# Attention block, one core: the first three groups' probabilities by VectorE squares and transfers inside SBUF, the last stage's pools in another order, the gates' low parts one block sooner

## The chip, the cores and the metric

The kernel runs on one core of a Trainium2 chip. The metric is the device time of one execution in microseconds, the median of several. The engines are named as in the profile: PE (TensorE) multiplies matrices, DVE (VectorE), ACT (ScalarE) and POOL (GpSimd) work on tiles, SP (SyncE) issues most of the DMAs; POOL issues some of them too. PEld is the loading of weights into PE.

## The reference, cut to what matters

One layer over 4096 prompt rows (and 64 sample rows) of width 1024:

```
h = rmsnorm(x, g_pre);  z = h @ w_in                     # 2816 columns
cb, cc, ch, cg, q, k, v, ag, mq, mg = split(z)
out_a = silu(cg) * cb * conv3(cc * ch)                    # 256 columns
out_b = silu(ag) * window_attention(q, k, v, sink)        # 8 heads, 2 kv heads, window 128
out_c = silu(mg) * memory_attention(mq, mk, mv)           # 4 heads, 256 memory tokens
y = concat(out_a, out_b, out_c) @ w_out
x + rmsnorm(y, g_post)
```

The window attention goes by groups of 128 queries: group b sees the keys of its own 128 rows and of the 128 rows before (none for group 0), and a sink per head. All arithmetic keeps float32 accuracy: a product is made from high and low parts in three matmuls.

## The kernel before, in words

Four stages follow one another. In phases 0, 1 and 2 (`input_projection`) z is computed for blocks of 520 rows; in each block seven Strassen products (A11 to A22 in `PRODUCTS`), each over all column tiles of the phase, give the `c` matmuls of L374. The first two blocks of phase 0 are plain (`plain_block`, `plain_jobs`, eight steps each). Jobs are put between the products: loads, splits of the operands (`hi_x` on ACT, `lo_x` on DVE, L364 and L365), evictions (L381, L383, L417). PE, DVE and SP take their instructions in the order in which the program lists them.

Phase 2 has eight blocks of seven products, counted by n in `third_jobs(b, p)`: up to n = 12 the memory's keys and values, from n = 13 `first_chunk`, and then the attention of groups 0, 1 and 2, in pieces put between products. `wo_load` and `wo_split` in its last block bring w_out and split it into high parts (ACT) and low parts (DVE, `w_split`, L197).

The last stage is opened by `open_attention` (L1013), which makes its pools, and runs 32 prompt blocks and one block of the samples. A block is 48 `y` matmuls (out-projection of 128 rows), and between them, at places given by `events_of(i)`, the attention of the group three blocks ahead: scores (`ws`, `xs`), softmax, and the values (`pv`) of the group one block ahead. Groups come in chunks of two: `chunk_load(c)` loads a chunk's keys (`kst`) and queries (`q`) by POOL's DMA queue, `load_mix` its gates from `md` by SP's, for even chunks into `place`, for odd ones into `mix`.

A group's probabilities have queries in partitions; the values need keys there. For groups from 3 on the scores lie as squares of 32 columns: `turn_band` and `turn_cross` transpose 32x32 squares on DVE (STREAM_TRANSPOSE 128x1024 each), 16 DMAs of 32x512 on SP (`w<-s`, L1274) move the squares inside SBUF, `masks` zeroes what the window excludes (four affine selects on POOL, L1283), and `values` makes 32 matmuls: 16 for the memory (`pv<-w,mv`), 8 for the band (`pv<-w,vh`), 8 for its rest (`pv<-wd,vh`). The score buffer `s` of odd groups is single.

For groups 0 to 2 the probabilities are flat, and PE transposes them: 8 transposes for the band (`wt`), 8 for the memory (`xt`), copies out of PSUM on ACT or DVE (`wpt`, `xpt`, `w`), affine selects on POOL (L1296, L1298), then `early_values` with `wo` matmuls of 128x512 and 16 `xo` matmuls. Group 2's transposes stand in block 0 of the last stage, its values in block 1.

Further places that the change touches: `rows_product` (L311) spreads the normalisation factors of a block over partitions by PE, and ACT copies them to `rb` (L317); `rows_load` (L262) loads the factors of phase 1's first two blocks; `Block.split` (L1573, L1578) makes a block's high part `mh` on ACT and low part `ml` on DVE; the sample's window attention is done in four pieces among blocks 27 to 30.

## Time and profile before

| | us |
|---|---|
| median of 3 runs | 1496.32 (1494.26 to 1496.76) |
| profiled execution | 1497.36 |
| its span | 1495.6 |
| phase 2 begins, ends | 676.1, 953.5 |
| a block of the last stage without waits | 16.0 |

The profiled execution took 1.76 us beside its span, and 1.04 more than the median. Times in a timeline count from the span's start. A row such as "805.46 0.59 ACT L1292 COPY wpt<-wt 128x512 ..." gives the start, the duration, the engine, the line of the kernel, the operation, the tiles written and read, and in brackets, where there is one, the idle time before it with its inferred releaser. A row of a group gives the count, the busy time and the mean duration in ns, then the idle time. A row of the windows gives for each engine the busy time and the number of instructions, in the order PE, PEld, DVE, ACT, POOL, then the granted PE clock, the share of the DMA engines in use and GB/s. Matmuls overlap: what a piece of PE costs is read from its start to the start of the next.

### The profile page before, as it was taken

Reading aid. Unit: us, or ns where it says so; the run is one execution under the profiler, and the core shown is the slowest. Engines: PE = TensorE matmul, PEld = TensorE weight load, DVE = VectorE, ACT = ScalarE, POOL = GpSimd, SP = SyncE. Lnnn points to the kernel's source line nnn. Section 1 sums busy time; section 2 is a strip of 40 time slices with the busy share of each in tenths; the row PEclk is TensorE's granted clock in tenths of the full one; section 3 lists DMA queues with packets and bytes.
Section 4 is the critical chain, followed back from the end, with each engine's and each line's share of the span. In section 5 each row is a group of like instructions: output and inputs, shape, how many; then the busy total and the mean of one; then the engine's idle time right before and its main releaser. Section 6 shows DMA issues by size and latency. Waiting matters only on the chain.

```text
span 1495.6 us, 30807 instructions
## 1 busy us (share of the span) xinstructions
PE 1470.5 (98%) x11479; PEld 1343.0 (90%) x11479; DVE 1202.6 (80%) x1887; ACT 763.3 (51%) x1879; POOL 412.7 (28%) x553
## 2 busy tenths in 40 slices
PE   9999999999999999999999999999999999999998
PEld 9999999999999999999999999877777777778766
DVE  5779888898988877798667767968898888898853
ACT  5776655566422222244444534755655565665542
POOL 0222322212400000000000011235555656566631
PEclk9999999999999999999999999999999999999999
DMA  9989999886765432377967797989889998989662
GB/s 259 168 253 228 289 263 272 232 294 238 188 225 171 156 112 103 124 264 247 317 227 218 222 272 244 305 242 239 220 220 249 234 238 222 223 220 248 191 201 99
DMA packets 212363, 334.18 MB, mean 223 GB/s; under 512 B 54517, under 2 KB 126197, under 8 KB 212181
## 3 DMA queue, kind: packets, MB, share of 16 engines
q1 hardware_dynamic: 170117, 259.30, 57.8%
q0 software_dynamic: 40800, 69.76, 19.3%
q10 hardware_dynamic: 1296, 3.15, 0.7%
q8 instruction: 91, 1.49, 0.4%
q14 instruction: 59, 0.48, 0.1%
HBM read 192.54 MB, written 110.15 MB: 202 GB/s over the span
## 4 chain that ended last, share of the span: by engine, by line
PE 73%; DMA 11%; DVE 7%; issue 4%; SPq 3%; ACT 2%; POOL 1%; ACTq 0%; DVEq 0%; POOLq 0%
PE c L374 43%; PE y L66 19%; PE pv L66 4%; PE ws L66 2%; DMA nat<-in_x_p 2%; SPq L1274 2%; DMA place<-in_xt 2%; PE y L1601 1%; DMA place<-md 1%; PE xs L66 1%; DMA wr_3A<-in_w_in 1%; DMA o_yp<-xr 1%; DMA xr<-in_x_p 1%; PE mem_acc L790 1%; DMA md<-th 1%
## 5 line engine op out<-in xcount | busy, mean ns | idle before, releaser
L66 PE MATMUL y<-wo,mh 128*128 128x512 f32 x992 | 318.3, 395 | 0.0
L381 DVE TENSOR_TENSOR z<-c,z 128x520 f32<-128x520 f32 (+1 forms) x308 | 194.1, 643 | 84.5 <-PE c L374 83.9
L66 PEld LDWEIGHTS y<-wo,mh 128*128 128x128 f32 x992 | 186.3, 188 | 52.2 <-DVE wmx L66 5.0
L66 PE MATMUL y<-wo,ml 128*128 128x512 f32 x496 | 193.5, 390 | 1.0 <-DVE ml L66 1.0
L1211 ACT ACTIVATE s<-s,wnm 128x128 f32<-128x128 f32 x248 | 96.0, 388 | 41.9 <-DVE wnm L66 38.9
L66 PEld LDWEIGHTS y<-wo,ml 128*128 128x128 f32 x496 | 93.3, 188 | 19.5 <-DVE ml L66 1.4
L1236 POOL TENSOR_SCALAR s<-s,xrd 128x256 f32<-128x256 f32 x124 | 59.7, 497 | 156.5 <-DVE xrd L66 101.5
L1194 ACT COPY s<-ws 128x256 f32<-128x256 f32 x124 | 40.0, 377 | 96.5 <-PE ws L66 70.9
L1629 POOL TENSOR_TENSOR xr<-yn,xr 128x1024 f32<-128x1024 f32 x30 | 72.1, 2402 | 25.4 <-ACT yn L1628 22.4
L66 DVE STREAM_TRANSPOSE s<-s 128x1024 f32<-128x1024 f32 x58 | 70.9, 1236 | 3.0 <-POOL s L1236 3.0
L749 POOL MEMSET negs<- 128x1 f32 x1 | 0.1, 99 | 264.8 <-PE c L374 264.8
L1609 ACT ACTIVATE y<-y 128x512 f32<-128x512 f32 (+1 forms) x64 | 37.4, 584 | 54.0 <-DVE yn L66 46.6
L1283 POOL TENSOR_SCALAR_AFFINE_SELECT wd<-w 128x512 f32<-128x512 f32 (+1 forms) x56 | 51.7, 923 | 42.2 <-DMA w<-s 32.9
L66 DVE TENSOR_TENSOR yn<-y,gpost 128x512 f32<-128x512 f32 x62 | 42.3, 682 | 24.2 <-PE y L66 22.1
L1228 ACT ACTIVATE s<-xs,xnm 128x256 f32<-128x256 f32 x124 | 56.5, 462 | 4.1 <-DVE xnm L1226 3.2
L66 DVE COPY_PREDICATED s<-wmask,ws 128x256 f32<-128x256 uint8 x116 | 44.9, 441 | 16.2 <-ACT s L1194 10.4
L66 PEld LDWEIGHTS ws<-kst,q 64*128 64x128 f32 x696 | 44.5, 190 | 12.8 <-issue 10.2
L287 ACT ACTIVATE nat<-nat 104x1024 f32<-104x1024 f32 x40 | 42.2, 1057 | 25.9 <-DMA nat<-in_x_p 25.8
L66 PE MATMUL ws<-kst,q 64*128 64x256 f32 x696 | 51.1, 292 | 2.0 <-DMA q<-qd 1.9
L383 ACT COPY z<-c 128x520 f32<-128x520 f32 (+1 forms) x44 | 24.4, 554 | 51.8 <-PE c L374 48.8
L1628 ACT ACTIVATE yn<-yn,yst 128x1024 f32<-128x1024 f32 x31 | 35.6, 1150 | 24.9 <-POOL yst L1622 22.9
L415 ACT CAST zh<-z 128x520 fp32r<-128x520 f32 x56 | 33.3, 624 | 26.4 <-DVE z L381 22.6
(1013 smaller groups left out, 4995.6 us busy)
## 6 DMA issues: line engine op xcount, KB each, us to landing
w<-s SPq DMA_DIRECT2D x464, 64.0 KB
q<-qd POOLq DMA_DIRECT2D x32, 768.0 KB, 9.7
xr<-in_x_p SPq DMA_DIRECT2D x32, 512.0 KB
nat<-in_x_p SPq DMA_DIRECT2D x39, 416.0 KB
o_yp<-xr SPq DMA_DIRECT2D x31, 512.0 KB
md<-th POOLq DMA_DIRECT2D x48, 260.0 KB, 6.2
qd<-zh SPq DMA_DIRECT2D x48, 260.0 KB
qd<-z SPq DMA_DIRECT2D x48, 260.0 KB
```

Of the source, the lines that this page charges most:

```text
L66: return (lambda *args, **kw: tc.keep_in_program_order(fn(*args, **kw))) if on else fn
L287: S.activation(t[:RG], t[:RG], AF.Square, accum_out=r[:RG, i : i + 1])
L374: TE.matmul(bank[:, :HW], l, r, start=first and i == 0, stop=last and i == 3 * KH - 1)
L381: add = lambda dst, other: V.tensor_tensor(dst, c, other, op=ALU.add)
L1194: S.copy(to, squares(s3[:, :, P : 2 * P]))
L1211: S.activation(sm[:, h], sm[:, h], AF.Exp, bias=nm[:, h : h + 1], scale=SCALE, accum_out=den[:, h : h + 1])
L1228: S.activation(p[:, i], s[:, i].rearrange("p (a k j) -> p a k j", a=2, k=4), AF.Exp, bias=nm[:, i : i + 1], scale=SCALE, accum_out=den[:, ...
L1236: G.tensor_scalar(p[:, i], p[:, i], rd[:, i : i + 1], 0.5, op0=ALU.mult, op1=ALU.mult)
L1283: G.affine_select(out, src, pattern=[[32 * sign, 2], [0, 8], [sign, 32]], compare_op=op, fill=0.0, base=base * sign, channel_multiplier=-s ...
L1609: square = lambda acc=acc, p=p, c0=c0, c1=c1, end=end: S.activation((psum(2, "sq") if end else acc)[:m, : c1 - c0], acc[:m], AF.Square, sc ...
L1628: tc.keep_in_program_order(S.mul(yn, yn, st[:, 3:4]))
L1629: G.tensor_tensor(self.xr, yn, self.xr, op=ALU.add)
```

## The change

Groups 0 to 2 take the way of the other groups: squares, `turn_band` and `turn_cross` on DVE (together `early_turn`), 16 DMAs, `masks`, `values`. Their DMAs go by POOL's queue. A timetable `EARLY` says at which n of phase 2 each piece stands: group 0 has its scores from 15 to 18, its turn at 20, masks at 24, values at 26; group 1 scores 25 to 28, then 30, 34, 36; group 2 scores 36 to 39, turn 41, masks 45, and its values stay in block 1 of the last stage. Groups 0 and 1 write their values to two PSUM banks and multiply the gates in three pieces instead of two.

The low parts of wo for j = 9, 11, 13, 15 are made by POOL. Chunk 1 is loaded at n = 29. Chunk 3 is loaded in block 1 of the last stage and no longer in block 0, and `kst2` lies in another pool. The pools of the last stage are made in another order, so new tiles lie where other old tiles were and wait for other instructions; on SP the first load of x now stands ahead of the load of chunk 1's gates, which stood far ahead of it. In block 0, group 3's scores come at place 3 instead of 4. POOL keeps the listed order in blocks 1 and 2. From block 28 on the split of the next block moves from (1, 3) to (0, 6). `rows_product(2)` moves to the front of its step; `rows_load` of phase 1's second block moves from p = 1 to p = 0.

```diff
-    def w_split(w, raw):
+    def w_split(w, raw, engine=V):
         copy = S.copy(w[:, 0], raw)
...
-        V.tensor_tensor(w[:, 1], raw, f(w[:, 0]), op=ALU.subtract)
+        engine.tensor_tensor(w[:, 1], raw, f(w[:, 0]), op=ALU.subtract)
...
-        if p == 1 and nph == 1 and nb < PLAIN_BLOCKS:
+        if p == (0 if nb else 1) and nph == 1 and nb < PLAIN_BLOCKS:
             jobs.append(lambda: rows_load(nb, nb > 0))
...
-            (1, 5): lambda: [*fills(2, "S3"), lambda: rows_product(2), *fills(2, "S1"), *gains(2, "B21"), *fills(2, "S4"), *row],
+            (1, 5): lambda: [lambda: rows_product(2), *fills(2, "S3", "S1"), *gains(2, "B21"), *fills(2, "S4"), *row],
...
-        if n > 13 and third["chunk"]:
-            jobs.append(third["chunk"].pop(0))
-        elif n > 13 and len(chunks) == 1:
+        if n == 29:
             jobs.append(lambda: chunk_load(1))
-        elif n > 13 and early[0] < 4 and n >= 38:
-            if early[0] == 0:
-                groups[2] = Group(chunks[1], 0)
-            jobs.append(lambda u=early[0]: groups[2].early_scores(u))
-            early[0] += 1
+        for b, at in enumerate(EARLY):
+            if n == at[0]:
+                jobs.append(lambda b=b: groups.update({b: Group(chunks[b // 2], b % 2)}))
+            for fn in [fn for fn, m in zip(PIECES, at) if m == n]:
+                jobs.append(lambda b=b, fn=fn: fn(groups[b]))
...
+    EARLY = ((15, 16, 17, 18, 20, 24, 26), (25, 26, 27, 28, 30, 34, 36), (36, 37, 38, 39, 41, 45))
+    PIECES = (*(lambda g, n=n: g.early_scores(n) for n in range(4)), lambda g: g.early_turn(), lambda g: g.masks(), lambda g: g.values())
...
-        w_split(wo[k][h], wo_raw.pop(j))
+        w_split(wo[k][h], wo_raw.pop(j), G if j > 8 and j % 2 else V)
...
-        yq = ctx.enter_context(tc.tile_pool(name="yq", bufs=1, side="right"))
         vp = ctx.enter_context(tc.tile_pool(name="vp", bufs=4, side="right"))
-        yp = ctx.enter_context(tc.tile_pool(name="yp", bufs=2, side="right"))
-        bq = att.enter_context(tc.tile_pool(name="bq", bufs=1))
-        wp = att.enter_context(tc.tile_pool(name="wp", bufs=2))
-        wl = att.enter_context(tc.tile_pool(name="wl", bufs=1))
-        bp = att.enter_context(tc.tile_pool(name="bp", bufs=1))
-        mixp = att.enter_context(tc.tile_pool(name="mixp", bufs=1))
+        left = lambda name, bufs=1: att.enter_context(tc.tile_pool(name=name, bufs=bufs))
+        sp, bp, wd0 = left("sp"), left("bp"), left("wd0")
+        left("gap").tile([P, NS], F32, name="gap")
+        bq, yq, wl, wd1, mixp, yp = left("bq"), left("yq"), left("wl"), left("wd1"), left("mixp"), left("yp", 2)
+        wp = wd0, wd1
...
-            if c == 2:
-                self.kst = third["work"].tile([P, D], F32R, tag="u", name="kst2")[:, : 2 * (P + CT)].rearrange("p (a n) -> p a n", a=2)
-            else:
-                self.kst = self.pool().tile([P, 4, P + CT], F32R, tag="k", name=f"kst{c}")[:, :2]
+            odd = c == 0 or c % 2
+            self.kst = self.pool().tile([P, 2 if odd else 4, P + CT], F32R, tag="k", name=f"kst{c}")[:, :2]
...
         def turn_cross(self):
             part = self.squares[:, :, 256:]
-            tc.keep_in_program_order(V.transpose(part, part))
-            to = (wl if self.b % 2 else wp).tile([P, 4, 512], F32, tag="w", name=f"w{self.b}", bufs=1)
+            self.in_turn(V.transpose(part, part))
+            b = self.b
+            to = (wl if b % 2 and b > 1 else third["we"]).tile([P, 4, 512], F32, tag="w", name=f"w{b}")
             for g in range(4):
                 for k in range(4):
-                    DMA.dma_start(to[32 * k : 32 * k + 32, g], self.squares[32 * g : 32 * g + 32, k])
+                    (DMA if b > 2 else G).dma_start(to[32 * k : 32 * k + 32, g], self.squares[32 * g : 32 * g + 32, k])
...
+        def early_turn(self):
+            self.turn_band()
+            self.turn_cross()
...
-        if i == 2:
-            chunk_load(4)
+        if i in (1, 2):
+            chunk_load(i + 2)
...
-            at(0, 0, lambda: groups[2].transposes(0))
-            at(0, 3, lambda: groups[2].transposes(1))
             at(1, 0, weights, 3)
...
-        at(0, 0 if i else 4, values_and_scores, i)
+        at(0, 0 if i else 3, values_and_scores, i)
...
-            if i != 2:
-                at(0, 1 if i else 4, chunk_load, i // 2 + 3)
+            if i > 2:
+                at(0, 1, chunk_load, i // 2 + 3)
...
-                at(1, 3, blocks[i + 1].split)
+                at(*((1, 3) if i < 28 else (0, 6)), blocks[i + 1].split)
...
-        InOrder.on, InOrder.scalar, InOrder.gpsimd = i < 31, i == 0, i == 2
+        InOrder.on, InOrder.scalar, InOrder.gpsimd = i < 31, i == 0, i in (1, 2)
```

Removed with it: `early_transposes`, `transposes`, `band_transposes`, `cross_transposes`, the former `early_values` of a group and its flat branches in `open_scores`, `band_weights`, `cross_values` and `values`. Not shown: some loads of the last stage's opening that move by a place, and the sample's mask and value tiles, which lie in other pools.

More of the change, by code (lines that the diff above doesn't have):

```diff
@@ L862, in first_chunk @@
         third["work"] = right.enter_context(tc.tile_pool(name="work", bufs=1, side="right"))
+        third["we"] = right.enter_context(tc.tile_pool(name="we", bufs=1, side="right"))
         chunk_load(0)
@@ L865, in first_chunk @@
         chunk.load_mix()
-        third["chunk"] = [chunk.early_values]
-        for i in range(2):
-            pair = Group(chunk, i)
-            third["chunk"] += [lambda pair=pair, n=n, fn=fn: fn(pair, n) for fn, ns in (
-                (Group.early_scores, (0, 1, 2)), (Group.early_transposes, (0, 1)), (Group.early_values, (1,)),
-                (Group.early_scores, (3,)), (Group.early_transposes, (2, 3)), (Group.early_values, (3,))) for n in ns]
+        chunk.early_values()
     sums_at = {(0, 3 + i): pair for i, pair in enumerate(PHASES[1])}
@@ L1645, in hybrid_layer @@
     chunk_load(2)
-    for n in range(1, 4):
+    for n in range(2, 4):
         half_load(n)
```

150 lines of the change are left out of this document (47 added, 103 removed).

## The prediction

> **What bounds the kernel now.** I read the busy times first, then the matrix engine's (PE's) idle pieces in the timeline, then the windows of five microseconds around the opening of the last stage, then the chain of waits there.
>
> ```profile
> PE 1470.5 (98%) x11479; PEld 1343.0 (90%) x11479; DVE 1202.6 (80%) x1887; ACT 763.3 (51%) x1879; POOL 412.7 (28%) x553
> ```
>
> PE sets the end. A microsecond is won only by PE work taken out, by a PE wait that goes, or by full clock where it is now reduced. These are the PE waits that the change touches (number in front: when PE went on; in brackets: how long it had waited and for whom):
>
> ```profile
> 89.64 0.39 PE L374 MATMUL c<-hi_1B,w_2A 128*128 128x260 f32 x1 [2.40 <-ACT rb L317]
> 377.97 0.39 PE L374 MATMUL c<-lo_0B,w_0S 128*128 128x260 f32 x1 [0.40 <-DVE lo_0B L365]
> ...
> 804.79 0.63 PE L1291 MATMUL wt<-ident,s 128*128 128x128 f32 x4 [0.85 <-PE c L374]
> 858.41 0.63 PE L1291 MATMUL wt<-ident,s 128*128 128x128 f32 x4 [0.24 <-DVE s L1220]
> 909.25 0.39 PE L374 MATMUL c<-lo_6T,w_0S 128*128 128x260 f32 x1 [0.73 <-DVE lo_6T L365]
> 972.08 2.72 PE L66 MATMUL ws<-kst,q 64*128 64x256 f32 x22 [1.92 <-DMA q<-qd]
> 994.97 1.09 PE L66 MATMUL pv<-w,mv 128*64 128x128 f32 x16 [2.88 <-ACT y L1609]
> ...
> 1439.31 0.50 PE L66 MATMUL y<-wo,ml 128*128 128x512 f32 x1 [1.04 <-DVE ml L66]
> ```
>
> The two near 972 and 995 cost more than their idle time. In the windows the column after the busy times is the granted clock, then the DMA share:
>
> ```profile
> 970.00:975.00 5.00, 3.08 (x28) 2.93 (x28) 3.09 (x6) 1.51 (x5) 1.14 (x4) 0.71 1.23 350
> 975.00:980.00 5.00, 5.00 (x41) 3.26 (x39) 3.63 (x8) 4.13 (x17) 2.28 (x2) 0.95 1.17 370
> ...
> 995.00:1000.00 5.00, 4.96 (x35) 2.66 (x36) 3.26 (x8) 3.15 (x13) 3.67 (x5) 0.66 0.67 192
> ```
>
> Lost clock is the window times what the clock lacks: 5 × 0.29 + 5 × 0.05 = 1.7 us behind the first wait, 5 × 0.34 = 1.7 behind the second. So the first is worth 1.92 + 1.7 = 3.6, the second 2.88 + 1.7 = 4.6. The Trainium skill ("TensorE: Matmul & The Clock Gate", What's actually happening) says that the clock falls after at least one idle window of about 3.4 us; the trace differs, since waits of 1.92 and 2.88 us are each followed by a reduced clock. By that rule the two waits would be worth 4.8 us, not 8.2, and the forecast below about 2 us later; the rows decide.
>
> What ends the two waits:
>
> ```profile
> 958.60 1.70 POOL L1095 DMA_DIRECT2D q<-qd  x2 [27.88 <-DMA qd<-z]
> ...
> 993.75 1.51 POOL L1283 TENSOR_SCALAR_AFFINE_SELECT wd<-w 128x512 f32<-128x512 f32 x2 [8.46 <-DMA w<-s]
> 995.33 1.41 POOL L1283 TENSOR_SCALAR_AFFINE_SELECT w<-w 128x512 f32<-128x512 f32 x2
> ...
> 993.67 0.65 ACT L1194 COPY s<-ws 128x256 f32<-128x256 f32 x2 [6.84 <-DMA w<-s]
> ```
>
> ```profile
> 970.99 15.37 DMA place<-md
> ```
>
> The queries q2 are issued by POOL only at 958.60, into a full DMA (shares above 1), and arrive when PE has waited for them until 972.08. The second wait is a row of three: the load place<-md, 15.37 us long in the chain of waits, holds up the transfers w<-s of group 3 behind it on SP; ACT's score copy waits for them until 993.67 because it writes the buffer they read; PE waits for ACT's square behind that copy.
>
> **The change part by part.** *PE work of groups 0 to 2.* These rows give starts, so a piece lasts to the next row's start:
>
> ```profile
> 814.93 1.08 PE L1054 MATMUL wo<-wpt,mix_s 128*64 128x512 f32 x4
> 815.94 0.39 PE L374 MATMUL c<-hi_4B,w_0A 128*128 128x260 f32 x1
> ...
> 833.95 1.09 PE L1054 MATMUL xo<-xpt,mv 128*64 128x128 f32 x16
> 834.97 0.39 PE L374 MATMUL c<-hi_4T,w_2S 128*128 128x260 f32 x1
> ...
> 864.56 1.08 PE L1054 MATMUL wo<-s,mix_s 128*64 128x512 f32 x4
> 866.43 0.39 PE L374 MATMUL c<-hi_5T,w_2S 128*128 128x260 f32 x1
> ...
> 953.52 1.03 PE L66 MATMUL wt<-ident,s 128*128 128x128 f32 x8
> 954.39 0.60 PE L66 MATMUL xt<-ident,s 128*128 128x128 f32 x4
> 954.75 0.48 PE L66 MATMUL y<-wo,mh 128*128 128x512 f32 x1
> ...
> 975.81 1.09 PE L66 MATMUL pv<-w,mv 128*64 128x128 f32 x16
> 978.55 0.50 PE L66 MATMUL y<-wo,mh 128*128 128x512 f32 x1
> ...
> 1109.48 1.09 PE L66 MATMUL pv<-w,mv 128*64 128x128 f32 x16
> 1112.12 0.50 PE L66 MATMUL y<-wo,mh 128*128 128x512 f32 x1
> ```
>
> Sixteen transposes per group: eight take 954.39 − 953.52 = 0.87, four 0.36, so 0.87 + 2 × 0.36 = 1.59. Values now: group 0 takes 1.01 + 1.02 = 2.03, group 1 1.87 + 1.02 = 2.89, group 2 2.74. After, each group does what group 12 does at 1109.48, 2.64. Savings: 3.62 − 2.64 = 0.98; 4.48 − 2.64 = 1.84; 4.33 − 2.64 = 1.69. Together **−4.5**. With the transposes go the waits ahead of them, 0.85 + 0.24: **−1.1**.
>
> *What takes the transposes' place.* Per group two 128x1024 block transposes on DVE, 16 transfers inside SBUF issued by POOL, four masks on POOL. Rows of before for these, and for phase 2 as a whole:
>
> ```profile
> L66 DVE STREAM_TRANSPOSE s<-s 128x1024 f32<-128x1024 f32 x58 | 70.9, 1236 | 3.0 <-POOL s L1236 3.0
> 685.00:953.00 268.00, 265.66 (x2179) 256.10 (x2178) 197.39 (x312) 130.64 (x257) 20.06 (x26) 1.00 0.81 256
> L1095 POOL DMA_DIRECT2D q<-qd x30: 821/842/870, 718.4 to 1354.9; - x30
> ```
>
> DVE gains 6 × 1.24 = 7.4 us and is busy 197.39 of 268 us there, so it has room on the mean; each pair is still 2.5 us in front of whatever DVE does next, and the operand splits lo_x stand in that queue (909.25 shows PE waiting 0.73 for one). I charge one more wait of that size, **+0.6**; ends 0 and 7.4, all of it on the path. POOL is busy 20.06 of 268 us. Its issues take 0.84 each: 16 × 0.84 = 13.4. From the turn to the values the timetable leaves six products of about 5 us (some 54 in 268 us), 30 us; less 2.5 for the transposes, one product for DVE's queue, and 1.51 + 1.41 for the masks, about 20 us are left for 13.4. Hidden, at 0; if not, PE stands, because its order is fixed.
>
> The Trainium skill speaks against this move ("SBUF — State Buffer", SBUF: two separate sides): a DMA issued from GpSimd has its descriptors written by that engine, which is locked out while certain VectorE operations hold the shared port; it names 620 ns becoming 3100. The row of 30 issues agrees with no such thing: 821 to 870 ns, through phase 2 and the last stage, beside a DVE that is 74% busy. With 3100 ns the sixteen would take 50 us and PE would come about 30 us late twice; that is the third rival.
>
> *First wait of the last stage.* The order on POOL now has q2 ahead of kst2, without the wait for wo's splits on DVE that stands ahead of it now (the row of 958.60 names an older store), and chunk 3's loads behind block 0 instead of beside it. PE needs q2 at about 967 to 968, one set of transposes sooner than 972.08 − 1.92 = 970.16. Issued near 954 to 957 with the same 13 us it lands at 967 to 970, with less beside it sooner. I take the whole **−3.6**; ends −3.6 and 0. New here: kst2 comes behind q2, and four 128x512 splits of wo go to POOL, where the nearest row is a 128x1024 sum of 2.4 us:
>
> ```profile
> L1629 POOL TENSOR_TENSOR xr<-yn,xr 128x1024 f32<-128x1024 f32 x30 | 72.1, 2402 | 25.4 <-ACT yn L1628 22.4
> ```
>
> Half of it is 1.2 each; they are wanted by the second half of y, over 5 us into the block. I take 0; ends 0 and 4 × 1.2 = 4.8.
>
> *Second wait.* The first mix<-md and the xr loads of before on SP:
>
> ```profile
> L1103 SPq DMA_DIRECT2D mix<-md x8: 403/406/447, 961.3 to 1426.7; - x8
> ```
>
> ```profile
> 970.09 0.81 SPq L1558 DMA_DIRECT2D xr<-in_x_p  x2
> ```
>
> SP now issues xr0, then the mix of chunk 1, xr1, place, then w<-s. Group 3's softmax starts sooner (four copies on ACT and four splits on DVE fewer ahead of it), and place meets less traffic; but the load of mix, issued 9 us ahead of xr0 before, now stands directly ahead of it, and PE comes about 6 us sooner (the first wait's 3.6, 1.6 of transposes, and the values). The two nearly cancel. Ends −4.6 (gone) and 0; I take **−2.0**.
>
> *Small moves.* Phase 0's row product is now PE's first job, and the ACT copy rb goes ahead of one cast:
>
> ```profile
> 88.50 0.60 ACT L193 CAST w_2S<-wa2A 128x512 fp32r<-128x512 f32 x1
> 89.01 0.58 ACT L317 COPY rb<-rows_y 128x520 f32<-128x520 f32 x1
> ```
>
> That is 0.51 of the 2.40: **−0.5**. The row load of phase 1's second block stands about 2 us earlier on SP; it held DVE here, and PE behind it:
>
> ```profile
> 375.52 1.24 DVE L341 TENSOR_TENSOR x_1B<-x_1B,rb 128x1040 f32<-128x1040 f32 x1 [2.59 <-DMA rb<-rowd]
> ```
>
> PE's waits after it begin with 0.40 at 377.97 and are small and several; **−0.8**, ends −1.6 and 0. The low parts of the last prompt blocks come half a block sooner, which removes PE's wait for ml at 1439.31: **−1.0**. What they push back is the sample's softmax.
>
> The sum: −4.5 − 1.1 + 0.6 − 3.6 − 2.0 − 0.5 − 0.8 − 1.0 = −12.9. The profiled execution took 1497.36, 1.04 above the median of 1496.32, so 1497.36 − 12.9 − 1.04 = **1483.4 us**.
>
> **The rivals.** *The opening only exchanges its waits (0.25).* Against the forecast speak the DMA shares above 1 until 980 and the 15.37 us of one load: mix 1 is issued 9 us later than before and its gate multiply stands in DVE's order; if it too takes 15 us from 971 it lands near 986, and DVE and what follows are held. For it speaks that total bytes are unchanged. Then −3.6 and −2.0 are lost and up to 5 us are added: 1489.0 to 1494, taken as 1490.5. In this case the change does not do at the opening what its order says.
>
> *DVE becomes the bound of phase 2 (0.10).* It decides where a transposing pair meets a split lo_x that is due; all 7.4 us in place of 0.6 gives 1490.2. The 71 us of DVE idle time in the window speak against.
>
> *POOL's transfers come late (0.15): the slower side.* Place: PE's fixed order at the values of groups 0 and 1. It decides once one issue takes over 20 / 16 = 1.25 us. If a 1.24 us DVE operation holds up each 0.84 us issue, sixteen take 33.3, PE is 13 us late twice and loses 1.7 of clock each time: +29.4, so 1512.8. About 1.7 us per issue would already eat the whole gain.
>
> **How the numbers follow.** The forecast has 0.50. What a measurement can tell from no change is 0.2%, 3 us. Forecast: all faster. Exchange: 0.18 faster, 0.07 same. DVE: 0.06 faster, 0.04 same. POOL: slower. So 0.74, 0.11, 0.15. Low end: the second wait gone wholly (−2.6) and the row load's other 0.8 and a little of the charge of 0.6 bring 1479.5; high end: the exchange with nearly its whole addition, 1494. For the likeliest case alone 1479.5 to 1488.
>
> **What would show it.** No transposes and no idle before them at 805 and 858; PE's values of groups 0 and 1 with no wait for POOL; 16 POOL issues of w in under 14 us; the scores of block 1 starting without a wait for q; granted clock 1.00 behind it; a wait of 1 to 2 us for group 3 some 9 us earlier than 995; the row product's wait at 1.9. It is wrong if PE waits at the values in phase 2, or if DVE stands for the mix of chunk 1 until past 980.

## The result, and the profile after

The changed kernel is slower: 1501.97 us, median of 7 runs (1499.18 to 1508.01), beside 1496.08 for the kernel before (7 runs, 1494.26 to 1496.76). The ratio is 1.005, with a 95% interval of 1.0032 to 1.0067. The profiled execution took 1505.62, which is 3.65 above the median, and the two profiled executions, on which the sums below rest, lie 8.26 apart, while the medians lie 5.9 apart: the sums overstate the loss by some 2.4 us.

The busy times of the page of after answer to the first line of the prediction:

```profile
PE 1470.2 (98%) x11459; PEld 1343.8 (89%) x11459; DVE 1211.9 (81%) x1889; ACT 758.0 (50%) x1869; POOL 441.8 (29%) x607
```

By the page's count PE lost twenty instructions, and the span grew by 8.3. Where, is read from the windows by stage: phases 0 and 1, phase 2, the opening of the last stage up to the scores of block 5, the middle up to those of block 28, and the rest. Columns: window, length, busy time and instructions of PE, PEld, DVE, ACT and POOL, granted clock, DMA share, GB/s. After:

```profile
0.00:669.18 669.18, 665.13 (x5499) 663.26 (x5499) 554.60 (x762) 326.14 (x546) 104.10 (x166) 1.00 0.74 216
669.18:954.96 285.78, 277.58 (x2243) 267.50 (x2244) 214.02 (x336) 132.50 (x260) 52.26 (x83) 0.98 0.81 256
954.96:1041.46 86.50, 79.02 (x551) 62.92 (x549) 72.06 (x129) 47.92 (x175) 41.43 (x54) 0.98 1.05 269
1041.46:1413.77 372.31, 371.13 (x2689) 291.69 (x2688) 330.78 (x581) 222.44 (x808) 218.65 (x276) 1.00 0.89 225
1413.77:1503.90 90.13, 77.34 (x486) 58.42 (x485) 40.47 (x85) 29.01 (x82) 25.35 (x30) 0.94 0.44 141
```

The same windows of the kernel before:

```profile
0.00:676.14 676.14, 667.53 (x5499) 663.45 (x5499) 553.78 (x762) 325.12 (x546) 105.25 (x166) 1.00 0.73 214
676.14:953.52 277.38, 275.04 (x2255) 265.48 (x2255) 206.77 (x330) 135.10 (x265) 20.50 (x27) 1.00 0.80 253
953.52:1042.22 88.70, 83.76 (x559) 65.59 (x557) 70.71 (x133) 51.20 (x181) 41.61 (x55) 0.96 0.97 256
1042.22:1413.34 371.12, 370.17 (x2688) 291.88 (x2688) 329.85 (x580) 222.78 (x808) 220.17 (x275) 1.00 0.89 226
1413.34:1495.60 82.26, 73.98 (x486) 56.62 (x485) 41.52 (x85) 29.12 (x82) 25.16 (x32) 0.99 0.49 157
```

Idle time is the length less PE's busy time; lost clock is summed from windows of 5 us, each with 5 times what its clock lacks.

| stage | predicted | measured | of it PE idle | of it lost clock |
|---|---|---|---|---|
| phases 0 and 1 | −1.3 | −7.0 | −4.6 | 0 |
| phase 2 | −2.8 − 1.1 + 0.6 = −3.3 | +8.4 | +5.9 | +5.2 |
| opening | −1.7 − 3.6 − 2.0 = −7.3 | −2.2 | +2.5 | −1.7 |
| middle | 0 | +1.2 | +0.2 | 0 |
| end | −1.0 | +7.9 | +4.5 | +5.2 |
| sum | −12.9 | +8.3 | +8.6 | +8.7 |

What is left is 8.3 − 8.6 − 8.7 = −9.0. About 1.8 of it only corrects a double count: in after, windows over the waits themselves show that the clock was reduced by 1.41 us during the wait that ends at 1461.12, by 0.30 during the one at 943.54 and by 0.14 during the one at 994.47, where a slow clock costs nothing more. The other 7.2 or so is less PE work; 4.5 of it was counted from rows of work taken out, for the rest there is no row (ends of matmuls are modelled). So the work went as hoped, and more than all of it was paid back in waits and in the clock behind them. These are the waits, from PE's timeline of after (start, duration, what, and in brackets the idle time before it with its releaser), with the first row of group 0's values ahead of them:

```profile
832.04 1.09 PE L1046 MATMUL pv<-w,mv 128*64 128x128 f32 x16
...
863.62 0.39 PE L374 MATMUL c<-lo_5T,w_0S 128*128 128x260 f32 x1 [0.77 <-DVE lo_5T L365]
...
870.58 0.39 PE L374 MATMUL c<-lo_5B,w_0S 128*128 128x260 f32 x1 [2.36 <-DVE lo_5B L365]
...
941.65 0.39 PE L374 MATMUL c<-hi_7B,w_0S 128*128 128x260 f32 x1 [0.87 <-ACT hi_7B L364]
...
943.54 0.59 PE L374 MATMUL c<-lo_7B,w_0S 128*128 128x260 f32 x1 [1.51 <-DVE lo_7B L365]
...
971.31 1.70 PE L66 MATMUL ws<-kst,q 64*128 64x256 f32 x24 [2.69 <-issue]
...
994.47 1.76 PE L66 MATMUL pv<-w,mv 128*64 128x128 f32 x14 [4.79 <-DMA w<-s]
...
1461.12 1.97 PE L66 MATMUL pv<-w,vh 128*64 128x256 f32 x8 [5.87 <-POOL w L1248]
```

And the windows of after behind them, the granted clock third from the right:

```profile
870.00:875.00 5.00, 4.42 (x24) 4.42 (x25) 1.77 (x2) 0.95 (x1) 1.57 (x3) 0.66 1.08 288
...
940.00:945.00 5.00, 2.63 (x14) 2.22 (x13) 5.00 (x9) 3.57 (x5) 0.78 (x1) 0.79 1.03 381
945.00:950.00 5.00, 5.00 (x25) 5.00 (x25) 5.00 (x6) 2.62 (x5) 3.93 (x2) 0.52 0.50 174
...
1455.00:1460.00 5.00, 0.24 (x6) 0.00 (x1) 0.21 (x1) 1.84 (x3) 3.87 (x4) 0.84 0.27 100
1460.00:1465.00 5.00, 3.88 (x18) 1.84 (x19) 0.78 (x2) 0.00 (x0) 1.75 (x3) 0.50 0.37 125
```

The two small waits near 942 and 944, 2.38 us together, come with 5 × 0.21 + 5 × 0.48 = 3.45 of lost clock, 0.30 of it inside the second wait.

**What did not happen.** POOL's transfers are early. Its timeline for group 0:

```profile
810.79 6.99 POOL L1234 DMA_DIRECT2D w<-s  x14 [5.61 <-DVE s L1229]
...
824.19 1.54 POOL L1248 TENSOR_SCALAR_AFFINE_SELECT wd<-w 128x512 f32<-128x512 f32 x2 [4.04 <-DMA w<-s]
825.70 1.40 POOL L1248 TENSOR_SCALAR_AFFINE_SELECT w<-w 128x512 f32<-128x512 f32 x2
```

One issue takes 6.99 / 14 = 0.50 us, not the 0.84 assumed; the masks are done at 827.1 and PE begins the values at 832.04 without a wait. The transposes and their two waits are gone, and the 32 matmuls of a group take 2.48 us (832.04 to 834.52), a little under the 2.64 predicted.

**Where DVE is late in phase 2.** The wait at 870.58 is for `lo_5B`. DVE's timeline of after:

```profile
866.70 2.08 DVE L381 TENSOR_TENSOR z<-c,z 128x520 f32<-128x520 f32 x4 [2.79 <-PE c L374]
868.70 0.70 DVE L851 STREAM_TRANSPOSE vq<-vl 128x512 f32<-128x512 f32 x1
869.33 1.20 DVE L365 TENSOR_TENSOR lo_5B<-x_5B,hi_5B 128x1040 fp32r<-128x1040 f32 x1
```

ACT's timeline of after, for the high part it needs:

```profile
865.90 1.06 ACT L364 CAST hi_5B<-x_5B 128x1040 fp32r<-128x1040 f32 x1 [3.61 <-DMA x_5B<-hd_B]
```

And DVE's timeline of before, for the same piece of work:

```profile
874.63 1.23 DVE L365 TENSOR_TENSOR lo_5B<-x_5B,hi_5B 128x1040 fp32r<-128x1040 f32 x1
...
876.01 0.70 DVE L853 STREAM_TRANSPOSE vq<-vl 128x512 f32<-128x512 f32 x1
876.64 0.66 DVE L381 TENSOR_TENSOR z<-c,z 128x520 f32<-128x520 f32 x1
...
877.34 1.35 DVE L381 TENSOR_TENSOR z<-c,z 128x520 f32<-128x520 f32 x3
```

In after the split's input is there at 866.96, DVE had stood idle for 2.79 us until 866.70, and yet the split starts at 869.33: in the listed order it now stands behind four evictions and the transpose `vq` of the values, while before it stood ahead of all five. It starts 869.33 − 866.96 = 2.37 late, which is PE's whole wait of 2.36. DVE has room; what changed is who stands behind whom. SP's timeline of after has a similar row on the way of the load:

```profile
855.52 3.24 SPq L855 DMA_DIRECT2D vn<-vq  x4
858.81 2.33 SPq L525 DMA_DIRECT2D x_5B<-hd_B  x1
```

The stores `vn`, which wait for an earlier `vq`, take SP 3.24 us ahead of the load of `x_5B`. But they stood ahead of it before as well, at 2.29, so only about 1 us of this is new.

**Block 7.** Its two waits cost more than block 5's: 0.87 + 1.51 + 3.45 = 5.83, less the 0.30 counted twice, beside 0.77 + 2.36 + 1.70 = 4.83. Here it is a load that is late. SP issues `x_7B` at 932.63, behind six loads of w_out, and ACT, done with six casts of w_out, stands idle for 0.71 us until it has landed and begins its high part at 940.54. Issuing the six loads took SP 5.72 us, against 4.05 before; POOL issues group 2's transfers at the same time, from 920.39 to 930.10. DVE starts the low part at 942.26, behind two splits of wo, though the high part is ready at 941.60.

**Splits on POOL.** The four splits that left DVE saved it nothing. By line, before, then after (busy us, mean ns):

```profile
L197 DVE TENSOR_TENSOR wo<-wor,wo 128x512 fp32r<-128x512 f32 x16 | 10.6, 684 | 0.1
```

```profile
L197 DVE TENSOR_TENSOR wo<-wor,wo 128x512 fp32r<-128x512 f32 x12 | 11.6, 988 | 0.3 <-ACT wo L193 0.3
```

POOL's timeline of after has two of its four:

```profile
945.71 3.93 POOL L197 TENSOR_TENSOR wo<-wor,wo 128x512 fp32r<-128x512 f32 x2 [4.93 <-ACT wo L193]
```

So 1.96 us each for these two, not the 1.2 taken (the other two took 1.29 and 1.31), and DVE's own at 948.42 and 956.02, beside POOL's, took 1.77 and 2.16. The Trainium skill ("SBUF — State Buffer", Who interferes with whom) says that a VectorE instruction with both inputs in SBUF contends with a GpSimd instruction that reads SBUF. The trace agrees as far as DVE goes: its split at 956.02, beside POOL's from 956.31 to 957.62, took about three times the 684 ns that one took before. The prediction had weighed another section of the same page of the Trainium skill, on DMA issues that starve beside VectorE; of that the 48 issues show nothing.

**The end.** POOL's timeline of after before the wait of 5.87:

```profile
1456.06 0.55 POOL L1558 TENSOR_TENSOR yst<-yst,mhalf 128x1 f32<-128x1 f32 x1 [9.08 <-DVE yst L66]
1456.57 1.51 POOL L1248 TENSOR_SCALAR_AFFINE_SELECT wd<-w 128x512 f32<-128x512 f32 x2
1458.06 2.33 POOL L1565 TENSOR_TENSOR xr<-yn,xr 128x1024 f32<-128x1024 f32 x1
1460.35 1.40 POOL L1248 TENSOR_SCALAR_AFFINE_SELECT w<-w 128x512 f32<-128x512 f32 x2
```

And of before:

```profile
1451.53 1.52 POOL L1283 TENSOR_SCALAR_AFFINE_SELECT wd<-w 128x512 f32<-128x512 f32 x2 [4.85 <-DMA w<-s]
1453.11 1.41 POOL L1283 TENSOR_SCALAR_AFFINE_SELECT w<-w 128x512 f32<-128x512 f32 x2
1455.74 0.55 POOL L1622 TENSOR_TENSOR yst<-yst,mhalf 128x1 f32<-128x1 f32 x1 [1.22 <-DVE yst L66]
```

The masks of group 31, ahead of `yst` and `xr` before, now stand behind the one and on both sides of the other. POOL waits 9.08 us for a number of the block's norm that DVE has only at the block's end, and PE waits for the masks.

### The profile page after: what moved, and what is told of

Same layout as the page of the kernel before. It is cut to its first block, busy times and chain, and to the rows that moved or that the text cites. A ratio compares the mean times of both kernels' runs of the same rounds, so it can differ in the third digit from the quotient of the medians.

```text
span 1503.9 us, 30849 instructions
## 1 busy us (share of the span) xinstructions
PE 1470.2 (98%) x11459; PEld 1343.8 (89%) x11459; DVE 1211.9 (81%) x1889; ACT 758.0 (50%) x1869; POOL 441.8 (29%) x607
## 4 chain that ended last, share of the span: by engine, by line
PE 77%; DMA 6%; issue 6%; DVE 6%; ACT 2%; SPq 1%; POOL 1%; ACTq 0%; POOLq 0%; DVEq 0%
PE c L374 49%; PE y L66 18%; PE pv L66 4%; PE ws L66 2%; DMA w<-s 1%; PE xs L66 1%; DMA place<-md 1%; PE mem_acc L789 1%; SPq L1234 1%; ACT s L1193 1%; DMA x_5T<-hd_T 1%; DMA wr_3S<-sd6S 1%; DMA o_yp<-xr 1%; DMA vd<-v 1%; DMA x_7B<-hd_B 0%
## 5 line engine op out<-in xcount | busy, mean ns | idle before, releaser
L66 PEld LDWEIGHTS ws<-kst,q 64*128 64x128 f32 x696 | 43.1, 186 | 12.9 <-issue 12.9
L1248 POOL TENSOR_SCALAR_AFFINE_SELECT w<-w 128x512 f32<-128x512 f32 x60 | 48.9, 834 | 1.8
```

Source lines behind the costliest of these rows:

```text
L66: return (lambda *args, **kw: tc.keep_in_program_order(fn(*args, **kw))) if on else fn
L1248: G.affine_select(out, src, pattern=[[32 * sign, 2], [0, 8], [sign, 32]], compare_op=op, fill=0.0, base=base * sign, channel_multiplier=-s ...
```

## The experiments

Each is timed against the kernel before on the same chip; "tail" is the time from the scores of block 28 to the last matmul (75.85 before, 83.67 after), phase 2 was 277.38 and 285.78, the opening 88.70 and 86.50.

**e1_small.** The kernel before with both row moves:

```diff
-        if p == 1 and nph == 1 and nb < PLAIN_BLOCKS:
+        if p == (0 if nb else 1) and nph == 1 and nb < PLAIN_BLOCKS:
-            (1, 5): lambda: [*fills(2, "S3"), lambda: rows_product(2), *fills(2, "S1"), ...],
+            (1, 5): lambda: [lambda: rows_product(2), *fills(2, "S3", "S1"), ...],
```

> The kernel before with two of the change's moves alone: the row product first in its step, and the row load of phase 1's second block at p = 0. Theory: these two give all of the 7 us by which phase 2 starts sooner in the changed kernel (669.2 against 676.1), so the time is 1489 to 1491 and the waits of 2.40 us at 89.6 and of 2.59 us on DVE at 375.5 are gone. Rival: the prediction's sizes, 0.5 and 0.8 us (1495), the rest of the 7 us coming from the other pools and loads.

1491.25 beside 1495.45; ratio 0.9977 (0.9967 to 0.9987). The pair is worth 4.2 us (1.9 to 4.9 by the interval), not 1.3.

**e2_tail.** The changed kernel with the low parts back at (1, 3):

```diff
-                at(*((1, 3) if i < 28 else (0, 6)), blocks[i + 1].split)
+                at(1, 3, blocks[i + 1].split)
```

> The changed kernel with the split of blocks 29 and 30 back at its old place. Theory: the split at the new place delays the sample's softmax by 1.5 us, group 31's transfers with it, and in the listed order of POOL its masks then stand behind the yst and xr operations; back at the old place they stand ahead of them, the wait of 5.87 us at 1461 is gone and the time is 6.5 to 8 us less (1494 to 1495.5), with the 1.04 us wait for ml back. Rival: group 31's transfers are late for another reason (pools, DMA traffic), the wait stays over 4 us and the time within 2 us of the changed kernel's.

1501.81; ratio 1.0043 (1.0028 to 1.0058). In its profile the wait of 5.87 is gone and the tail is 78.06, with PE's wait for `ml` back (2.01 and 0.75), but the time hardly moves: its phase 2 took 287.48, 1.7 more than after. A miss in size: the two ratios differ by about 1 us, with an estimated interval from 4.5 in e2's favour to 2.4 against it, so the 4.8 that e5 finds below in the kernel before is not found again in the changed kernel's time. Why not is open.

**e3_split.** The changed kernel with all low parts of wo on DVE:

```diff
-        w_split(wo[k][h], wo_raw.pop(j), G if j > 8 and j % 2 else V)
+        w_split(wo[k][h], wo_raw.pop(j))
```

> The changed kernel with all low parts of wo on DVE again. Theory: POOL's subtracts and DVE's two-operand operations hold each other up (DVE's wo split took 2.16 and lo_7T 1.99 us beside them), and q2's second half waits behind POOL's last split; without them q2 and kst2 are issued 1 to 2 us sooner, the 2.69 us wait at 971 shrinks below 1 and the time is 2 to 4 us less (1498 to 1500). Rival: what holds q2 and kst2 is the full DMA, the wait at 971 stays over 2 us and the time within 1 us of the changed kernel's.

1500.64; ratio 1.004 (1.0026 to 1.0054), 1.3 below after, within the intervals of both. All sixteen splits on DVE now took 11.8 us, where twelve beside POOL's four took 11.6; so the move buys DVE next to nothing. PE's waits of the opening only change their places: 2.95 and 1.17 for the scores of block 1, 1.10 for group 3's values.

**e4_chunk.** The changed kernel with chunk 1 loaded at n = 33 instead of 29, to see whether its transfers delay `x_5B`:

```diff
-        if n == 29:
+        if n == 33:
```

> The changed kernel with chunk 1's keys and queries loaded at n = 33 instead of 29. Theory: the 1.9 MB of that load collide with the loads of x_5T and x_5B (landing 7 to 8.5 us after issue), so the waits of 0.77 and 2.36 us at 864 and 871 go and the time is 3 to 5 us less (1497 to 1499). Rival: the transfers of group 1 inside SBUF and the loads around them make the x loads late, the waits at 864 to 871 stay over 2 us in sum.

1503.68; ratio 1.0056 (1.0042 to 1.007). The waits near 864 and 871 are 0.77 and 2.35, as after. That theory fell.

**e5_tail_before.** The kernel before with the early split alone, the reverse of e2:

```diff
-                at(1, 3, blocks[i + 1].split)
+                at(*((1, 3) if i < 28 else (0, 6)), blocks[i + 1].split)
```

> The kernel before with one part of the change alone: the splits of blocks 29 and 30 at (0, 6). Theory: the split takes DVE and ACT ahead of the sample's softmax, group 31's transfers start 1.5 us later, and POOL's listed order puts its masks behind yst and xr: a wait of 4 to 6 us of PE at the values of group 31 and a reduced clock, 1.04 us for ml gained; the time is 3 to 7 us more than before. Rival: the tail of the changed kernel is made by its other parts; this one gains 1 us (1494 to 1495).

1500.76 beside 1495.93; ratio 1.0037 (1.0022 to 1.0051). One line costs 4.8 us; the wait of 5.87 stands in its profile, at 1460.30, and its tail is 82.81.

**e6_nodma.** The changed kernel with POOL copying instead of issuing the 48 transfers of groups 0 to 2. The transfers are left out, so the first 384 rows hold other values:

```diff
-                    (DMA if b > 2 else G).dma_start(to[32 * k : 32 * k + 32, g], self.squares[32 * g : 32 * g + 32, k])
+            if b > 2: ...
+            else:
+                G.tensor_copy(to, self.squares)
```

> The changed kernel without the 48 transfers of groups 0 to 2: one copy on POOL per group in their place, so the values of the first 384 rows are not the reference's. Theory that the transfers' traffic makes the x loads late: the waits at the operands 5T, 5B and 7B (7.4 us in sum in the changed kernel) fall under 3, the time is 4 to 7 us less. Rival, that the order of DVE and SP listed around them does it: lo_5B keeps its 2.35 us wait, since it stands behind four evictions there too, and the time is within 3 us of the changed kernel's.

1503.08; ratio 1.0048 (1.0035 to 1.0061). The waits at 5B and 7B are gone, but others stand in their place (1.45 for `lo_4B`, 1.56 and 1.45 for block 6), and phase 2 took 283.07, 2.7 less than after. The split of `lo_5B` is still late: its high part is ready at 867.32 and it starts at 870.73, behind the same evictions and `vq`; PE did not wait because group 1's values stood ahead of it. So the transfers are not what makes that split late. For block 7 the run excludes nothing: without the transfers its waits are gone, and the six w_out loads take SP 3.20 us instead of 5.72. The copies that POOL makes instead, 1.9 us each, are work of their own, so the time says little.

**e7_vturn.** The changed kernel with the values' loads and transposes (`vl`, `vq`, `vn`) one product sooner, so that `vq` and the stores behind it no longer stand ahead of a split:

```diff
-        if n >= 15 and n % 3 == 0 and n < 39:
-            jobs.append(lambda: v_load((n - 15) // 3))
-        if n >= 17 and n % 3 == 2 and n < 41:
-            jobs.append(lambda: v_turn((n - 17) // 3))
+        if n >= 14 and n % 3 == 2 and n < 38:
+            jobs.append(lambda: v_load((n - 14) // 3))
+        if n >= 16 and n % 3 == 1 and n < 40:
+            jobs.append(lambda: v_turn((n - 16) // 3))
```

> The changed kernel with the loads and transposes of the values' halves (vl, vq, vn) one product sooner. In this build no split lo_x stands behind evictions of the product before. Theory: the stores vn<-vq in SP's order hold back the loads x_5T and x_5B, and DVE's listed order around lo_5B costs the wait; both go, the waits of 0.77, 0.81 and 2.36 us at 863 to 873 fall under 1 in sum, and the time is 3 to 5 us less than the changed kernel's (1497 to 1499). Rival: DVE is simply short of time in phase 2 after the block transposes; the waits move to other splits and the time stays within 1.5 us.

1496.0 beside 1495.93; ratio 0.9999 (0.999 to 1.0008): 6 us won back. DVE's timeline of e7, to be held against after's at 866 to 869:

```profile
864.40 1.24 DVE L365 TENSOR_TENSOR lo_5B<-x_5B,hi_5B 128x1040 fp32r<-128x1040 f32 x1 [0.39 <-ACT hi_5B L364]
866.21 2.21 DVE L381 TENSOR_TENSOR z<-c,z 128x520 f32<-128x520 f32 x4 [0.56 <-PE c L374]
```

The split is ahead of the four evictions again and PE's waits there are gone. The edit also let SP issue `x_5B` ahead of the stores `vn`, so it does not part the two. Not all of the 6 us is this: phase 2 fell by 4.4 to 281.38, with waits of 3.51 and 1.64 left in block 7, and the tail fell by 5.5 to 78.14, since `yst` now came between the masks at 1449 and PE waited 2.88 for them. The opening took 1.6 more (waits of 4.26 and 2.91).

**e8_three.** e7 with e2's and e3's edits.

> The changed kernel with three parts mended: values' halves one product sooner, the splits of blocks 29 and 30 back, all low parts of wo on DVE. Theory: the three losses add up and are independent, so 1490 to 1494, under the kernel before. Rival: PE, when it comes sooner, meets the same loads at the opening and in block 7 of phase 2, and the time is 1497 or more.

1492.74; ratio 0.9977 (0.9969 to 0.9986), 3.3 below e7. What is left in phase 2 (280.90) is in block 7: a wait of 3.75 for `hi_7T` and one of 1.28 for `lo_7T`. PE's timeline of e8:

```profile
933.73 0.42 PE L374 MATMUL c<-hi_7T,w_0S 128*128 128x260 f32 x1 [3.75 <-ACT hi_7T L364]
```

And ACT's:

```profile
932.10 0.62 ACT L193 CAST wo<-wor 128x512 fp32r<-128x512 f32 x1 [0.22 <-DMA wor<-in_w_out]
932.62 1.05 ACT L364 CAST hi_7T<-x_7T 128x1040 fp32r<-128x1040 f32 x1
```

`x_7T` is issued at 918.68, beside group 2's transfers (915 to 926), and has landed at 928.43, when SP's next load into the same tile goes. Its high part begins only at 932.62, because ACT has three casts of w_out listed ahead of it (929.62, 931.26, 932.10), and each waits for its load. The first of these loads was issued at 920.44 and is used 9.2 us later; in the kernel before, which lists them in the same order, it is 5.6, and PE does not wait there. So it is the listed order again, this time on ACT, and behind it loads that group 2's transfers slow.

**e9_group2.** e8 with group 2 four products sooner, `EARLY[2] = (32, 33, 34, 35, 37, 43)`.

> e8_three with group 2's pieces four products sooner in phase 2 (scores 32 to 35, turn 37, masks 43), so its 16 transfers are over before the loads of w_out begin. Theory: these transfers and the first six loads of w_out make x_7T land 12 us after its issue; without them beside it PE's waits at 7T (3.75 and 1.28 us in e8_three) fall under 1.5 in sum and the time is 3 to 5 us less (1488 to 1490). Rival: the loads of w_out alone, ahead of x_7B and x_7T on SP, make the wait; it stays over 3 us.

1494.22 beside 1496.43; ratio 0.9982 (0.9966 to 0.9999). The wait of 3.75 in block 7 is gone (the first w_out load is used 5.7 us after its issue), but the scores of group 2 wait 4.58 for chunk 1's queries at 861.18, and phase 2 is as long (281.03).

**e10_place.** e8 with POOL issuing the first `place<-md`, to test the prediction's row of three at the second wait:

```diff
-            DMA.dma_start(self.mix, md[:, :, self.ts].rearrange("k p n -> p k n"))
+            (G if self.c == 2 else DMA).dma_start(self.mix, md[:, :, self.ts].rearrange("k p n -> p k n"))
```

> e8_three with the load of chunk 2's gates into place issued by POOL in block 1 instead of by SP ahead of group 3's transfers. Theory: the transfers w<-s on SP wait for the landing of place (12.5 us in the changed kernel); without it they end 4 us or more sooner, the wait at group 3's values (3.54 us) falls under 1 and the time is 3 to 5 us less (1488 to 1490). Rival: the transfers themselves are slow in the full DMA; they still end past 984, the wait stays over 2.5 us.

1493.79; ratio 0.9984 (0.9971 to 0.9997), no gain over e8. SP begins with w3's transfers at 966.62 and still takes 14.59 us over them (17.53 in after), and PE waits 3.40 for them. What the queue waits for, from the waits of SP between 964 and 992 (us in total, times, longest), in after:

```profile
SPq L1234 <- DMA place<-md: 3.9, 1, 3.9
```

And in e10:

```profile
SPq L1234 <- DMA xr<-in_x_p: 2.8, 1, 2.8
```

`place` does hold the transfers of `w` up, by 6.0 us in the kernel before, 3.9 in after and 3.4 in e8: the prediction's row of three is right. With `place` out of the way, the loads that then stand ahead, `xr` (2.8) and the gates of chunk 1 (0.8), hold them about as long. So it is loads that are not down yet ahead of the transfers, and taking one of them away only brings up the next.

**e11_both.** e9 and e10 together.

> Both of the last two changes on e8_three. Theory: they add up, 1484 to 1488, which is the prediction's size reached with the losses taken out. Rival: what is won before the opening is waited for there, 1489 or more.

1496.29; ratio 0.9997 (0.9984 to 1.001). The opening took 84.59, the shortest of all, but the wait for chunk 1's queries is 5.77 in its profile. Its time above both parents was not expected and is not explained further.

**e12_group2_later.** e8 with group 2 only so much sooner that its transfers are over before block 7's loads, `EARLY[2] = (34, 35, 36, 37, 38, 45)`.

> e8_three with group 2's scores at 34 to 37, its turn at 38 and masks at 45: late enough for chunk 1's queries (whose wait spoilt e9_group2: 4.58 us at 861), and its transfers still ahead of the loads of w_out. Theory: no wait at 7T and none for q at 861, phase 2 takes 276 to 277.5 us instead of 280.9, and the time is 1488 to 1490. Rival: what phase 2 gains, the opening loses, since its loads and stores end no sooner: 1491 or more with a longer wait at the scores of block 1.

1490.94 beside 1496.95; ratio 0.9967 (0.9952 to 0.9982): 6 us below the kernel before and 11 below the changed kernel's median. Phase 2 took 277.66. PE's timeline of e12 has one wait above 0.7 us in that phase behind its first matmul:

```profile
857.23 0.43 PE L1046 MATMUL ws<-kst,q 64*128 64x256 f32 x1 [3.75 <-DMA q<-qd]
```

The first w_out load is used 5.2 us after its issue here. But PE also comes to block 7 later, by this wait (in e9 by the 4.58), so how much of block 7's cure is the loads' and how much the delay's is not shown.

**e13_rowprod** and **e14_rowload.** The kernel before with one of e1's two edits each.

> The kernel before with the row product of block 2 first in its step, nothing else. Theory: the wait for rb (2.40 us at 89.64) goes wholly, 1.5 to 2.5 us less than before. Rival: the prediction's 0.5.

> The kernel before with the row load of phase 1's second block at p = 0, nothing else. Theory: DVE's wait for rb (2.59 us at 375.52) goes and with it all of PE's small waits from 378 to 392, 1.5 to 3 us less than before; with the row product it adds up to the 4.2 of e1_small. Rival: the prediction's 0.8.

e13: 1493.65 beside 1495.9; ratio 0.9986 (0.9974 to 0.9999). e14: 1493.26; ratio 0.9982 (0.9966 to 0.9997). So 2.2 (0.1 to 3.9 by the interval) and 2.6 (0.4 to 5.1), which together make e1's 4.2 within their spread; neither interval excludes what the prediction gave its move, 0.5 and 0.8. DVE's timeline of e14 has no wait where the kernel before had 2.59:

```profile
369.97 1.24 DVE L341 TENSOR_TENSOR x_1B<-x_1B,rb 128x1040 f32<-128x1040 f32 x1
```

What such a wait costs differs between executions of the same code. DVE's was 2.59, 2.65 (e13), 3.97 (e5) and 2.28 (e15), and PE's behind it 0.40 in the kernel before and 2.31 with 1.75 of clock in e5. PE's wait for `rb` at the row product was 2.40 in the kernel before, but 0.68 in e5, e14 and e15, none of which touches it; with the move it was 0.48 (e13) and gone in e1.

**e15_order.** e5 with POOL held to the program's order in blocks 29 and 30, so that the split is early but the masks can't fall back:

```diff
-        InOrder.on, InOrder.scalar, InOrder.gpsimd = i < 31, i == 0, i == 2
+        InOrder.on, InOrder.scalar, InOrder.gpsimd = i < 31, i == 0, i == 2 or i in (29, 30)
```

> The kernel before with the splits of blocks 29 and 30 at (0, 6), as e5_tail_before, but POOL kept in the program's order in the blocks with index 29 and 30, so that group 31's masks stand ahead of yst and xr. Theory: the order alone makes the loss; the 5.87 us wait goes, the 1.04 for ml too, and the time is 0.5 to 1.5 us less than before. Rival: the late transfers make it; a wait of over 2 us for group 31 stays and the time is 2 us or more above before.

1494.43; ratio 0.9984 (0.9975 to 0.9994), 6.3 below e5. POOL's timeline of e15:

```profile
1451.03 1.51 POOL L66 TENSOR_SCALAR_AFFINE_SELECT wd<-w 128x512 f32<-128x512 f32 x2 [7.84 <-DMA w<-s]
1452.61 1.40 POOL L66 TENSOR_SCALAR_AFFINE_SELECT w<-w 128x512 f32<-128x512 f32 x2
1453.97 0.56 POOL L66 TENSOR_TENSOR yst<-yst,mhalf 128x1 f32<-128x1 f32 x1
```

The masks are ahead of `yst` again and the wait of 5.87 is gone; waits of 1.11 and 1.26 for group 31 and 1.70 of lost clock remain. Its profile was taken of its slowest execution, with a tail of 77.64 that is no shorter than before's 75.85, so it shows no gain from the early split; but tails of unchanged code also reach 77.49 (e13). The median lies 1.5 below the kernel before (0.9 to 3.7 by the interval), so a gain of the size of the −1.0 that the prediction gave this move, once the masks stay in place, is not excluded.

**e16_best.** e12 with the early split and POOL in order in blocks 1, 2, 29 and 30.

> e12_group2_later with the early splits of blocks 29 and 30 again and POOL in the program's order in the blocks with index 29 and 30. Theory: 1 to 3 us less than e12_group2_later, whose wait of 2.01 us for ml goes (1488 to 1490). Rival: group 31's transfers are late here, no gain or a loss.

1491.64; ratio 0.9974 (0.996 to 0.9989), no better than e12. Its tail is short (75.37), but the wait for chunk 1's queries was 5.12.

## Why the prediction was wrong, by its steps

The forecast was 1483.4 with a range of 1479.5 to 1494; the time lies 8 us above the range, on the other side of the kernel before.

- **PE work and transposes: right.** −4.5 and −1.1 rest on rows that came as read, with 2.48 us of values per group instead of 2.64.
- **POOL's transfers at 0: right at the values**, with issues of 0.50 instead of 0.84. The rival that was to make the kernel slower did not come; the kernel became slower in two other ways.
- **The charge of +0.6 for DVE in phase 2: the first step that failed.** It came from room on the mean and from one split seen late, and its upper end from the wrong mechanism, the new transposes themselves on the path. The phase lost 5.9 in waits and 5.2 in clock. e7 shows the first cause by moving it: a split that stands behind the evictions of the product before it and a transpose of the values. The edit had moved jobs between products and so changed the listed order of work it does not name. The second cost as much in the profile, 5.5 us: w_out's loads come late beside group 2's 16 transfers, and what is listed behind them, `x_7B` on SP here and `hi_7T` on ACT in e8, comes late with them. The rows of e8 show it, and in e9 and e12, where the transfers stand elsewhere, the loads are in time again (PE also comes later there). The prediction did not look there, since it costed the transfers by POOL's issues and not by what they delay. e4 and e6 exclude chunk 1's load and the transfers as cause of the first.
- **The opening's −3.6 and −2.0: failed**, in the way of the first rival. The scores of block 1 wait 2.69 instead of 1.92, since `kst2` now comes behind q2 and q2's second half behind a split on POOL (957.55, then 959.62 for `kst2`, which lands at 971.22 while both halves of q2 are there by 969.98). No clock was lost behind this wait, so it went from 3.6 to 2.7: 0.9 of the 3.6 came, for a reason that was not forecast. Group 3's values wait 4.79 instead of 2.88, with 1.75 of clock instead of 1.70: some 2 lost instead of won. Here the step that failed is that group 3's softmax would start sooner: its scores came 1.0 sooner (957.12 beside 958.15), but DVE was at the last evictions of z until 960.94 and began the softmax's work at 960.87, beside 960.74, and SP its transfers at 972.56, beside 972.44. PE came 2.4 sooner to values that were ready only 0.5 sooner. The stage gained 2.2, nearly the values' and transposes' 1.69. That `place` holds these transfers was right.
- **The end's −1.0: failed, by about 6 us.** e5 puts +4.8 on this one line. The prediction named what the move pushes back on its own engines, the sample's softmax, and left out that POOL's listed order would turn with it; e15, where POOL's order is held, takes the whole loss back. In the changed kernel e2 takes the wait out too, but its time shows a gain of only about 1 us. PE's wait for `ml` did go; whether that alone gains anything, e15 and e16 are too coarse to tell.
- **Row moves: right in kind, too small as a pair.** −1.3 measured −4.2 (e1), and 1.3 lies outside its interval of 1.9 to 4.9. −0.5 measured −2.2 (e13) and −0.8 measured −2.6 (e14), but each alone could be as predicted. Both were sized from one execution, in which PE waited 2.40 for the row product and 0.40 behind the row load; in other executions of the same code these were 0.68 and 2.31. In the profiled executions these phases differ by 7.0; with unchanged code they took 676.14, 674.80 (e5) and 672.29 (e15), so part of the 7 is chance.

## What to carry to other kernels

When a scheduler or pools decide the order, a job that is moved changes who stands behind whom on engines the edit doesn't name; compare the listed order on every engine around each moved job, and look for an instruction whose inputs come late (a norm's sum, an eviction) standing ahead of one that PE needs soon. Room on the mean says nothing of that: DVE had just been idle for 2.79 us when it ran four evictions and a transpose ahead of the split that was due. Cost a set of transfers by what they delay at the hour they run, not only by their issues: the loads beside them, and then the work listed behind those loads. And price a small wait from more than one execution, since unchanged code showed 0.40 and 2.31 for the same one.

## What the runs showed of the hardware

**The clock's price comes in pieces.** Behind waits the lost clock was 1.70 and 1.70 in the kernel before; in the changed one 1.70 (from 870), 3.45 (from 940), 5 × 0.09 + 5 × 0.26 = 1.75 (from 990), 5 × 0.24 + 5 × 0.11 = 1.75 (from 1425) and, with 0.10 of the window after the two shown, 3.40 (from 1455). The traces hold the moments at which the clock changes. Between 20 and 1482 us, the 18 profiles have 55 stretches of reduced clock, every one at 0.50, and they last 3.41 us (35 of them), 6.83 (18) or 10.24 (2), so one, two or three pieces that cost half of their length. One of two pieces, from after:

```profile
942.95:949.77 6.82, 6.22 (x28) 6.23 (x29) 6.82 (x9) 4.67 (x8) 3.93 (x2) 0.50 0.67 240
```

Within one execution they begin on a fixed grid: in after at 871.27, 942.95, 994.15, 1427.64 and 1458.36, which are 21, 15, 127 and 9 times 3.413 us apart. What counts is PE's idle time in the 3.413 us of the grid just before. In 54 of the 55 it was 1.56 us or more, and where the clock stayed full it was never above 1.83; in between both occur. So the same wait can cost nothing or a piece, by where it falls: the one of 2.69 us that ends at 971.31 is cut by the grid at 970.25 into 1.63 and 1.06 and lost nothing, while 0.87 and 1.51 close together, 1.78 of them in one step, lost two pieces. One case does not fit: 0.69 us at 1425.02 in after lost a piece, and the same 0.69 in the kernel before lost nothing. The Trainium skill ("TensorE: Matmul & The Clock Gate", What's actually happening) has the clock either full or half, set by windows of about 3.4 us; the stretches agree. That a window must be idle throughout does not agree: 2.36 us were enough at 870.58. So a wait is to be priced as its length and none, one or two pieces (seldom three), several small waits together can cost as much as a long one, and half clock that falls inside a wait costs nothing more.

**DVE's two-input work is slow beside POOL's**: 684 ns for a split on DVE before, 1.77 and 2.16 us beside POOL's in after, whose own took 1.29 to 2.28 us. No split of POOL's without DVE beside it was measured, so what DVE costs POOL is not shown.
